# The last down projection as seven products of 2x2 blocks, with its weight sums made in DRAM

## The chip, the cores and the metric

The kernel runs on one core of one Trainium2 chip. A core has a matrix engine (TensorE, PE in the profile; PEld is its loading of the stationary operand), a vector engine (VectorE, DVE), an engine for activations and copies (ScalarE, ACT), a general engine (GpSimd, POOL), an engine that here only issues transfers (SyncE, SP), and 16 DMA engines. The metric is the device time of one execution in microseconds (us), the median of several runs; lower is better.

## What is computed

A two-layer encoder on 272 tokens (16 learned meta tokens and 256 real ones) with 2048 channels, all in float32. Each layer mixes attention with a Fourier branch, then runs a feed-forward block with 5632 inner channels:

```python
for i in range(DEPTH):                                  # DEPTH = 2
    h = _rmsnorm(h_stream, norm_mix[i])
    proj = h @ w_in[i]                                  # q, k, v, f and two gates
    ...                                                 # attention and Fourier branch
    h_stream = h_stream + merged @ w_out[i]

    h2 = _rmsnorm(h_stream, norm_ffn[i])
    up = h2 @ w_up[i]                                   # 2048 -> 2 x 5632
    u_gate = _dwconv3_centred(up[..., :D_FF], w_conv[i], b_conv[i])
    u_val = up[..., D_FF:]
    h_stream = h_stream + (jax.nn.silu(u_gate) * u_val) @ w_down[i]
return h_stream[:, N_META:]                             # the meta tokens are dropped
```

The change concerns `@ w_down[1]`, the very last product. Of its result only the 256 real tokens are wanted.

## The kernel before

Activations are kept channel-major: a tile has 128 channels on the partitions and the tokens along the free dimension. `XT` is the residual stream (16 such tiles). A product is computed as three matmuls in a split format: every float32 operand is cut into a high part in the matrix engine's rounded format (`wh`, `xH`, `gH`) and the rest (`wl`, `xL`, `gL`), and high x high, high x low and low x high are added up in PSUM. Weights are stationary (128 x 128), tokens are moving.

All weights come from DRAM in chunks of 512 KB, 128 partitions x 4 blocks x 256 columns. The list `chunks` holds them in the order of use. For each, SyncE loads a `raw` buffer (four of them), ScalarE casts it to `wh` (`split_w`, L215) and VectorE subtracts to get `wl` (L217); there are three buffers of each, and `advance` keeps two chunks ahead of the one in use (`LOOK`). `group` (L246 to L280) takes the chunks of two output tiles and issues their matmuls: with three matmuls a block (L273 to L275), or, where two copies of the tokens fit into 512 columns, as two (L269: `wh` times high and low tokens side by side, 512 columns; L270: `wl` times high tokens, 256 columns). In layer 1 the value half of the up projection (`ps_uv`) and the down projection (`ps_d`) use the second form.

The small work between (norms, attention, transposes) is written as generators in a list `shadow`. `step()`, called after every second block of a group, lets one of them go on, so that this work is spread among the matmuls; `until` and `drain` force it. A scheduler then places the instructions of each engine: it keeps what the data and the buffers require, and may otherwise move an instruction ahead of others on its engine when it takes it to be ready. Each engine then works through its own list in that order. What must not move is wrapped in `keep_in_program_order`.

```python
def step(force=False):                        # L226
    for s in shadow:
        s[0] -= 1
    for s in list(shadow):
        if force or s[0] <= 0:
            try:
                s[0] = next(s[1])
            except StopIteration:
                shadow.remove(s)
            return
...
def pow_half(out, src):                       # L411
    n = src.shape[1]
    nc.gpsimd.tensor_tensor(out, src, mhalf[:, :n], op=ALU.pow)
```

POOL clears some buffers and takes the inverse square roots of the norms (`pow_half`, L413): `tok` for the norm of all channels, `rk` for the keys, `rq` for the queries, a few values each. VectorE turns `tok` and `rk` into diagonal blocks (`dg` L471, `dk` L829), which TensorE spreads over the partitions, and scales `rq` (L916).

The feed-forward block goes through its inner channels in two parts (`FF_SPLIT`, 24 and 20 tiles). For each pair of tiles: a group `ps_ug`, the convolution and the activation on VectorE and ScalarE, a group `ps_uv`, the product of both, and its split into `gH`, `gL`. After each part come eight groups of the down projection (`ps_d`), whose results VectorE adds to `XT` (L1148, L1154); in the last part of layer 1 the sum goes to a buffer `ot` (L1151) and out to DRAM, channel-major (L1152). While layer 0's feed-forward block runs, another generator (`prefold`) adds and subtracts halves of some weights of layer 1 on VectorE and keeps the results in DRAM (`fw`).

Of the kernel before, what the change touches and what calls it, by code (L numbers as in the profile page):

```python
# [16 lines left out]
P = 128  # L17
# [15 lines left out]
CW = 4  # L33
MG = 2
FF_SPLIT = (24, 20)
F0 = 1536

def _branch(text):
# [87 lines left out]


@with_exitstack
def encoder_kernel(ctx, tc, xT, params, consts, bmat, cfold, csign, w_fl, w_f64c, w_in, w_abr, w_four, w_f64, w_out, w_up, w_down, outT):
# [4 lines left out]

    dram = ctx.enter_context(tc.tile_pool(name="dram", bufs=1, space=bass.MemoryType.DRAM))
    fw = dram.tile([2 * KT, P, CW, MG * P], F32, name="fw")


    IN_F, IN_K, IN_V, IN_Q, IN_GA, IN_GF = 6, 4, 5, 0, 10, 18
    order = []  # L140
    for l in range(DEPTH):
        def g(w, mg, k0, k1):
            return [(w[l, mg, c], CW) for c in range(k0 // CW, k1 // CW)]
        if l == 0:
            f01 = [g(w_in, IN_F + i, 0, KT) for i in range(2)]
            order.append(((l, "f01"), [ch for pr in zip(*f01) for ch in pr]))
            for i in range(2, 4):
                order.append(((l, "f", i), g(w_in, IN_F + i, 0, KT)))
        order.append(((l, "k", 0), g(w_in, IN_K, 0, KT)))
        order.append(((l, "v", 0), g(w_in, IN_V, 0, KT)))  # L150
        for i in range(4):
            order.append(((l, "q", i), g(w_in, IN_Q + i, 0, KT)))
            if l == 1 and i == 1:
                order.append(((l, "f4"), [(fw[kt], CW) for kt in range(KT)]))
        for half in range(2):
            for kind, j in BRANCH_ORDER[half]:
                w, off, n = {"ga": (w_in, IN_GA, KT), "gf": (w_in, IN_GF, KT), "s": (w_four, 0, 8), "a": (w_abr, 0, 8)}[kind]
                chs = [(fw[KT + 2 * j + c], CW) for c in range(2)] if (l, kind) == (1, "s") else g(w, off + j, 0, n)
                order.append(((l, kind, j), chs))
            for mg in range(8):  # L160
                order.append(((l, "o", half, mg), g(w_out, mg, 8 * half, 8 * half + 8)))
        k0 = 0
        for c, n in enumerate(FF_SPLIT):
            for i in range(k0 // MG, (k0 + n) // MG):
                order.append(((l, "ug", i), g(w_up, i, 0, KT)))
                order.append(((l, "uv", i), g(w_up, FT // MG + i, 0, KT)))
            for mg in range(8):
                order.append(((l, "d", c, mg), g(w_down, mg, k0, k0 + n)))
            k0 += n
    chunks = [ch for _, chs in order for ch in chs]  # L170
    folded = {i for i, k in enumerate(k for k, chs in order for _ in chs) if k[:2] == (0, "s")}
    st = {"raw": 0, "fetch": 0, "next": 0, "grp": 0}
    raws, splits = {}, {}
    RAW, LOOK = 4, 2
# [62 lines left out]
    def until(hold, flag):  # L237
        while flag not in hold:
            step(True)

    def drain():
        while shadow:
            step(True)

    def group(key, rhs, width, tag="mm"):
        k, chs = order[st["grp"]]  # L246
        assert k == key, (k, key)
# [2 lines left out]
        ps = [psum.tile([P, 512], F32, tag=tag, name=f"ps_{nm}_{m}") for m in range(MG)]  # L250
        nk = CW * len(chs)
        for j in range(len(chs)):
            i = st["next"]
            advance(i + 1 + LOOK)
            pump(i)
            h, lo = splits.pop(i)
            st["next"] += 1
# [171 lines left out]
    def norm_in(m, goff):  # L429
        norm_split(m, goff)  # L430
        norm_sum(m)

    def prefold(pool):
        src = [w_fl[k] for k in range(KT)] + [w_four[1, j, c] for j in range(NG) for c in range(2)]
        outs = {}
        for j in range(len(src) + 1):
# [13 lines left out]
                outs[j] = o  # L450
            yield 1

    def norm_stats(holder, gap=0):
        am = small.tile([P, P // NM, NM], F32, tag="am", name="am", bufs=1)
        nc.vector.tensor_copy(am, _rep(acc[:, 0:NM], P // NM))
# [22 lines left out]
        holder["tok2"] = tok2  # L478

    xr = lambda lo: (lambda kt: (xH[:, kt, lo:T], xL[:, kt, lo:T]))  # L480

    for l in range(DEPTH):
        last = l == DEPTH - 1
# [615 lines left out]
        with tc.tile_pool(name=f"ffn{l}", bufs=1) as fp:  # L1099
            hold = {}  # L1100
            push(norm_stats(hold), 8)
            if not last:
                push(prefold(fp), 8)
            fused = 2 * W2 <= 512
            k0 = 0
            for c, n in enumerate(FF_SPLIT):
                gHL = fp.tile([P, FF_SPLIT[0], 2, T], F32R, tag="gHL", name="gHL")
                gH, gL = gHL[:, :, 0, :], gHL[:, :, 1, :]
                for i in range(k0 // MG, (k0 + n) // MG):
                    ps = group((l, "ug", i), xr(lo), W)  # L1110
                    until(hold, "tok2")
                    cs = []
                    for m in range(MG):
                        mt = 2 * i + m
                        wc = lambda t: prm[:, P_CW + (l * 3 + t) * FT + mt:P_CW + (l * 3 + t) * FT + mt + 1]
                        bc = prm[:, P_CB + l * FT + mt:P_CB + l * FT + mt + 1]
                        u = fp.tile([P, T], F32, tag="u", name="u", bufs=3)
                        nc.vector.tensor_tensor(u[:, lo:T], ps[m][:, :W], rstdB[:, lo:T], op=ALU.mult)
                        cv = fp.tile([P, T], F32, tag="cv", name="cv", bufs=4)
                        nc.scalar.activation(cv[:, lo2:T], u[:, lo2:T], AF.Identity, bias=bc, scale=wc(1))  # L1120
                        a = max(lo2, 1)
                        nc.vector.scalar_tensor_tensor(cv[:, a:T], u[:, a - 1:T - 1], wc(0), cv[:, a:T], op0=ALU.mult, op1=ALU.add)
                        nc.vector.scalar_tensor_tensor(cv[:, lo2:T - 1], u[:, lo2 + 1:T], wc(2), cv[:, lo2:T - 1], op0=ALU.mult, op1=ALU.add)
                        nc.scalar.activation(cv[:, lo2:T], cv[:, lo2:T], AF.Silu)
                        nc.vector.tensor_tensor(cv[:, lo2:T], cv[:, lo2:T], rstdB[:, lo2:T], op=ALU.mult)
                        cs.append(cv)
                    ps = group((l, "uv", i), (lambda kt: (xHL[:, kt, :, lo2:T],)) if fused else xr(lo2), W2)
                    for m in range(MG):
                        j = 2 * i + m - k0
                        cv = cs[m]  # L1130
                        val = ps[m][:, :W2]
                        if fused:
                            v = fp.tile([P, W2], F32, tag="v", name="v", bufs=2)
                            nc.scalar.copy(v, ps[m][:, W2:2 * W2])
                            nc.vector.tensor_tensor(v, v, val, op=ALU.add)
                            val = v
                        nc.vector.tensor_tensor(cv[:, lo2:T], cv[:, lo2:T], val, op=ALU.mult)
                        nc.scalar.copy(gH[:, j, lo2:T], cv[:, lo2:T])
                        nc.vector.tensor_tensor(gL[:, j, lo2:T], cv[:, lo2:T], gH[:, j, lo2:T].bitcast(F32), op=ALU.subtract)
                lastc = c == len(FF_SPLIT) - 1  # L1140
                for mg in range(8):
                    two = fused and not (lastc and mg == 7)
                    ps = group((l, "d", c, mg), (lambda kt: (gHL[:, kt, :, lo2:T],)) if two
                               else (lambda kt: (gH[:, kt, lo2:T], gL[:, kt, lo2:T])), W2)
                    for m in range(MG):
                        mt = 2 * mg + m
                        if two:
                            nc.vector.tensor_tensor(XT[:, mt, lo2:T], XT[:, mt, lo2:T], ps[m][:, W2:2 * W2], op=ALU.add)  # L1148
                        if last and lastc:
                            ot = fp.tile([P, SEQ], F32, tag="ot", name="ot", bufs=3)  # L1150
                            nc.vector.tensor_tensor(ot, XT[:, mt, NM:T], ps[m][:, :W2], op=ALU.add)  # L1151
                            nc.scalar.dma_start(outT[mt * P:(mt + 1) * P, :], ot)  # L1152
                        else:
                            nc.vector.tensor_tensor(XT[:, mt, lo2:T], XT[:, mt, lo2:T], ps[m][:, :W2], op=ALU.add)  # L1154
                            if lastc:
                                norm_in(mt, P_NM + (l + 1) * KT)
                k0 += n
            drain()


# [62 lines left out]
```

## Time and profile before

| | |
|---|---|
| median of 3 runs | 2576.59 us (2576.39 to 2577.74) |
| profiled execution, its own time | 2576.19 us |
| its span, first to last instruction | 2574.4 us |
| granted TensorE clock, mean | 1.000 |
| TensorE / VectorE / ScalarE / POOL busy | 2564.5 / 1726.7 / 1216.6 / 19.5 us |
| moved by DMA | 499.21 MB, 194 GB/s over the span |
| weight chunks split | 853 from `raw`, and 16 more from folded weights |
| last matmul starts | 2570.60 us |

Durations of matmuls in the profile overlap, since the engine is pipelined; the distance between two starts tells what one costs. A line number is that of the kernel before; in the changed kernel the same statements stand some 30 to 60 lines later. An arrow and a name in square brackets tell what ended an engine's idle time before an instruction.

### The profile page before, as it was taken

To read this page: it belongs to the slowest core of one execution; us is meant where nothing else is said; L and a number is where in the kernel's file an instruction comes from. 1 tells how busy PE (TensorE), PEld (TensorE's weight loads), DVE (VectorE), ACT (ScalarE), POOL (GpSimd) and SP (SyncE) were. 2 spreads that over 40 slices of the span, in tenths; PEclk is the share of its full clock that TensorE was granted. 3 is DMA by queue.
4 is the path that set the end of the run, shared out by engine and by line. 5 is a ranking of instruction groups with operands and counts; after the bars stand their busy time and mean duration, and the time that the engine had idled before them with its cause. 6 is when DMAs were issued, how large, how long until landed. Compare 5 with 4: busy or idle time off the path is not lost. (4 is left out here: it accounts for less than half of the span.)

```text
span 2574.4 us, 47883 instructions
## 1 busy us (share of the span) xinstructions
PE 2564.5 (100%) x19604; PEld 2500.8 (97%) x19604; DVE 1726.7 (67%) x2809; ACT 1216.6 (47%) x1766; POOL 19.5 (1%) x41
## 2 busy tenths in 40 slices
PE   9999999999999999999999999999999999999999
PEld 9999999999999999999999999999999998899988
DVE  7687766776666556666568877667766665566654
ACT  5455534554444334444446555445554443454443
POOL 0000000000000000000000000000000000000000
PEclk9999999999999999999999999999999999999999
DMA  6544555556666666666556445555555555555554
GB/s 235 166 152 160 189 181 186 186 205 223 227 226 225 228 226 227 226 214 218 175 173 221 150 147 197 192 191 196 181 186 184 187 188 188 185 184 188 184 198 158
DMA packets 143100, 499.21 MB, mean 194 GB/s; under 512 B 16400, under 2 KB 23440, under 8 KB 142880
## 3 DMA queue, kind: packets, MB, share of 16 engines
q1 hardware_dynamic: 140432, 494.02, 56.7%
q8 instruction: 153, 2.51, 0.4%
q10 hardware_dynamic: 2448, 2.13, 0.2%
q14 instruction: 67, 0.55, 0.1%
HBM read 474.43 MB, written 18.87 MB: 192 GB/s over the span
## 5 line engine op out<-in xcount | busy, mean ns | idle before, releaser
L217 DVE TENSOR_TENSOR wl<-raw,wh 128x1024 fp32r<-128x1024 f32 (+1 forms) x853 | 1037.7, 1218 | 708.4 <-ACT wh L215 703.0
L215 ACT CAST wh<-raw 128x1024 fp32r<-128x1024 f32 (+1 forms) x853 | 888.8, 1044 | 1052.0 <-issue 164.3
L274 PE MATMUL ps_ug<-xHL,wh 128*128 128x272 f32 (+1 forms) x1408 | 402.4, 286 | 0.0
L273 PE MATMUL ps_ug<-xHL,wh 128*128 128x272 f32 (+1 forms) x1408 | 402.0, 285 | 0.0
L275 PE MATMUL ps_ug<-xHL,wl 128*128 128x272 f32 (+1 forms) x1408 | 401.8, 285 | 0.0
L273 PEld LDWEIGHTS ps_ug<-xHL,wh 128*128 128x128 f32 x1408 | 265.4, 189 | 1.0
L274 PEld LDWEIGHTS ps_ug<-xHL,wh 128*128 128x128 f32 x1408 | 265.5, 189 | 0.1
L275 PEld LDWEIGHTS ps_ug<-xHL,wl 128*128 128x128 f32 x1408 | 265.0, 188 | 0.0
L269 PE MATMUL ps_uv<-xHL,wh 128*128 128x512 f32 x704 | 247.7, 395 | 0.0
L269 PE MATMUL ps_d<-gHL,wh 128*128 128x512 f32 x664 | 233.1, 395 | 0.0
L274 PE MATMUL ps_d<-gHL,wh 128*128 128x272 f32 (+1 forms) x744 | 214.4, 288 | 0.0
L273 PE MATMUL ps_d<-gHL,wh 128*128 128x272 f32 (+1 forms) x744 | 214.1, 288 | 0.0
L275 PE MATMUL ps_d<-gHL,wl 128*128 128x272 f32 (+1 forms) x744 | 214.0, 288 | 0.0
L274 PE MATMUL ps_uv<-xHL,wh 128*128 128x272 f32 x704 | 203.1, 288 | 0.0
L273 PE MATMUL ps_uv<-xHL,wh 128*128 128x272 f32 x704 | 202.9, 288 | 0.0
L275 PE MATMUL ps_uv<-xHL,wl 128*128 128x272 f32 x704 | 202.8, 288 | 0.0
L270 PE MATMUL ps_uv<-xHL,wl 128*128 128x256 f32 x704 | 197.7, 281 | 0.0
L270 PE MATMUL ps_d<-gHL,wl 128*128 128x256 f32 x664 | 186.5, 281 | 0.0
L269 PEld LDWEIGHTS ps_uv<-xHL,wh 128*128 128x128 f32 x704 | 132.4, 188 | 29.9
L269 PEld LDWEIGHTS ps_d<-gHL,wh 128*128 128x128 f32 x664 | 125.0, 188 | 29.2
L273 PE MATMUL ps_ga<-xHL,wh 128*128 128x272 f32 (+1 forms) x512 | 148.2, 289 | 0.0
L273 PE MATMUL ps_gf<-xHL,wh 128*128 128x272 f32 (+1 forms) x512 | 147.3, 288 | 0.0
(323 smaller groups left out, 5850.1 us busy)
## 6 DMA issues: line engine op xcount, KB each, us to landing
raw<-in_w_up SPq DMA_DIRECT2D x352, 512.0 KB, 3.5
raw<-in_w_in SPq DMA_DIRECT2D x191, 512.0 KB, 3.8
raw<-in_w_down SPq DMA_DIRECT2D x176, 512.0 KB, 3.5
raw<-in_w_out SPq DMA_DIRECT2D x64, 512.0 KB, 3.6
raw<-in_w_abr SPq DMA_DIRECT2D x32, 512.0 KB, 3.8
fw<-pfo SPq DMA_DIRECT2D x32, 512.0 KB, 4.3
raw<-fw SPq DMA_DIRECT2D x32, 512.0 KB, 4.3
raw<-in_w_four SPq DMA_DIRECT2D x16, 512.0 KB, 3.9
```

The lines of the kernel that those rows point to most:

```text
L215: nc.scalar.copy(h[:, a:b], r[:, a:b])
L217: nc.vector.tensor_tensor(lo[:, a:b], r[:, a:b], h[:, a:b].bitcast(F32), op=ALU.subtract)
L269: nc.tensor.matmul(o2, h[:, c, sl], ab, start=kt == 0, stop=False)
L270: nc.tensor.matmul(o, lo[:, c, sl], ab[:, 0, :], start=False, stop=kt == nk - 1)
L273: nc.tensor.matmul(o, h[:, c, sl], a, start=kt == 0, stop=False)
L274: nc.tensor.matmul(o, h[:, c, sl], b, start=False, stop=False)
L275: nc.tensor.matmul(o, lo[:, c, sl], a, start=False, stop=kt == nk - 1)
```

## The change

The down projection of layer 1 is no longer computed in two parts by weight-stationary groups.

- **Blocks.** The first 4096 of the 5632 inner channels (`KS` = 32 tiles) are cut in two halves of 16 tiles, the 256 tokens in two halves of 128, and the 2048 output channels in two halves of 1024. Four by four blocks are multiplied by seven products in place of eight, after Strassen and Winograd. Here the tokens are stationary (128 channels x 128 tokens) and the weights are moving, in two matmuls of 512 columns; so the output is token-major.
- **Sums of activations** are made by VectorE in place, and each set of four tiles of an operand is split on both engines when it is wanted (`make`).
- **Sums of weights**, needed in four of the seven products, are made in DRAM (`ft`) by the new generator `weight_sums`: 64 transfers of 1 MB issued by POOL, of which 32 copy and 32 add to what is there. It has a list of its own, `slow`: `step()` counts, starts it after 120 calls, and goes on after 28 more each time. The transfers are not wrapped in `keep_in_program_order`.
- **The rest**, 12 tiles of inner channels, is a plain token-stationary product (`tail`) in four blocks of 512 output columns. The 112 steps of the products (one chunk each) are interleaved: 58 among the chunks of the last six pairs of up tiles, 54 among the 24 chunks of the tail (`mix`).
- The residual is transposed to token-major (`res`) by TensorE during the first up tiles, and the sums are added to it. The output leaves token-major, so that the host no longer transposes it.
- The chunks of layer 1's down projection become 112 + 24 in place of 88. Layer 0 is computed as before.

```diff
+KS = 32
+NQ = KS // 2
+PRODUCTS = (0, 4, 5, 2, 6, 1, 3)
+TAIL_ORDER = (2, 3, 0, 1)
...
+    ft = dram.tile([4, NQ, P, CW, MG * P], F32, name="ft")
...
-        for c, n in enumerate(FF_SPLIT):
+        for c, n in enumerate(FF_SPLIT if l == 0 else (FT,)):
...
+    for b in TAIL_ORDER:
+        order.append(((1, "t", b), [(w_dt[b, j], CW) for j in range((FT - KS) // 2)]))
+    prods = {0: w_dn[0, 0:NQ], 1: w_dn[0, NQ:KS], 2: w_dn[1, NQ:KS], 3: ft[3], 4: ft[0], 5: ft[1], 6: ft[2]}
+    pchunks = [(prods[p][i], CW) for p in PRODUCTS for i in range(NQ)]
+    n_up, n_tail = (FT - KS) // MG * 2 * KT // CW, len(TAIL_ORDER) * (FT - KS) // 2
+    due = lambda t: 58 * t // n_up if t <= n_up else min(58 + (len(pchunks) - 58) * (t - n_up) // (n_tail - 2), len(pchunks))
...
+    slow = [120, None]
+
     def step(force=False):
+        if not force and slow[1]:
+            slow[0] -= 1
+            if slow[0] <= 0:
+                slow[0] = next(slow[1], None)
+                if slow[0] is None:
+                    slow[1] = None
...
+    def weight_sums():
+        rows = lambda ap: ap.rearrange("k p c m -> (k p) (c m)")
+        for j in range(NQ // 2):
+            a, b = 2 * j, 2 * j + 2
+            dst = lambda q: rows(ft[q, a:b])
+            w = lambda h, k: rows(w_dn[h, NQ * k + a:NQ * k + b])
+            for ops in ((((0, w(0, 0)), (2, w(1, 1)), (3, w(0, 1))), None),
+                        (((0, w(1, 0)), (2, w(1, 0))), ALU.add),
+                        (((1, None),), None),
+                        (((1, w(1, 1)),), ALU.add),
+                        (((3, dst(1)),), ALU.add)):
+                for q, src in ops[0]:
+                    if ops[1] is None:
+                        nc.gpsimd.dma_start(dst(q), dst(0) if src is None else src)
+                    else:
+                        nc.gpsimd.dma_start(dst(q), src, accum_op=ops[1], max_dma_last_dim=4096)
+                    yield 28
...
+    slow[1] = weight_sums()
...
+                def products():
...
+                    for n, p in enumerate(PRODUCTS):
+                        ps = [psum.tile([P, 512], F32, tag="aux", name=f"ps_p{p}") for _ in range(2)]
+                        for i in range(NQ):
+                            u = (n * NQ + i) // 4
+                            if i % 4 == 0:
+                                make(u + 2)
+                            wh, wl = (w.rearrange("p c m -> p (c m)") for w in next_split())
+                            a, b = made[u][:, 0, i % 4], made[u][:, 1, i % 4]
+                            for x, w in ((a, wh), (b, wh), (a, wl)):
+                                for h in range(2):
+                                    nc.tensor.matmul(ps[h], x, w[:, 512 * h:512 * h + 512], start=i == 0 and w is wh and x is a,
+                                                     stop=i == NQ - 1 and w is wl)
...
+                for b in TAIL_ORDER:
...
+                            for x, w in ((tH, wh), (tL, wh), (tH, wl)):
+                                nc.tensor.matmul(ps[r][:, :c1 - c0], x[:, kt, tk], w[:, q, c0:c1], start=kt == 0 and x is tH and w is wh,
+                                                 stop=kt == NT - 1 and w is wl)
...
-    args.append(nc.dram_tensor("outT", (D, SEQ), F32, kind="ExternalOutput").ap())
+    args.append(nc.dram_tensor("out", (SEQ, D), F32, kind="ExternalOutput").ap())
```

More of the change, by code (lines that the diff above doesn't have):

```diff
@@ L243, in drain, with next_split @@
             step(True)
+    def next_split():
+        i = st["next"]
+        advance(i + 1 + LOOK)
+        pump(i)
+        st["next"] += 1
+        return splits.pop(i)
     def group(key, rhs, width, tag="mm"):
@@ L252, in group @@
         for j in range(len(chs)):
[L253 to L257, printed above, removed]
+            for _ in range(mix.get((key, j), 0)):
+                next(st["products"])
+            h, lo = next_split()
             cm = [(c, m) for c in range(CW) for m in range(MG)]
@@ L1103, in encoder_kernel, with conv_gate, split_to @@
                 push(prefold(fp), 8)
-            fused = 2 * W2 <= 512
+            def conv_gate(i):
+                ps = group((l, "ug", i), xr(lo), W)
+                until(hold, "tok2")
+                cs = []
+                for m in range(MG):
+                    mt = 2 * i + m
+                    wc = lambda t: prm[:, P_CW + (l * 3 + t) * FT + mt:P_CW + (l * 3 + t) * FT + mt + 1]
+                    bc = prm[:, P_CB + l * FT + mt:P_CB + l * FT + mt + 1]
+                    u = fp.tile([P, T], F32, tag="u", name="u", bufs=3)
+                    nc.vector.tensor_tensor(u[:, lo:T], ps[m][:, :W], rstdB[:, lo:T], op=ALU.mult)
+                    cv = fp.tile([P, T], F32, tag="cv", name="cv", bufs=4)
+                    nc.scalar.activation(cv[:, lo2:T], u[:, lo2:T], AF.Identity, bias=bc, scale=wc(1))
+                    a = max(lo2, 1)
+                    nc.vector.scalar_tensor_tensor(cv[:, a:T], u[:, a - 1:T - 1], wc(0), cv[:, a:T], op0=ALU.mult, op1=ALU.add)
+                    nc.vector.scalar_tensor_tensor(cv[:, lo2:T - 1], u[:, lo2 + 1:T], wc(2), cv[:, lo2:T - 1], op0=ALU.mult, op1=ALU.add)
+                    nc.scalar.activation(cv[:, lo2:T], cv[:, lo2:T], AF.Silu)
+                    nc.vector.tensor_tensor(cv[:, lo2:T], cv[:, lo2:T], rstdB[:, lo2:T], op=ALU.mult)
+                    cs.append(cv)
+                return cs
+            def split_to(h, low, v):
+                nc.scalar.copy(h, v)
+                nc.vector.tensor_tensor(low, v, h.bitcast(F32), op=ALU.subtract)
             k0 = 0
-            for c, n in enumerate(FF_SPLIT):
+            for c, n in enumerate(() if last else FF_SPLIT):
                 gHL = fp.tile([P, FF_SPLIT[0], 2, T], F32R, tag="gHL", name="gHL")
@@ L1109, in encoder_kernel @@
                 for i in range(k0 // MG, (k0 + n) // MG):
[L1110 to L1126, printed above, removed]
@@ L1127, in encoder_kernel @@
-                    ps = group((l, "uv", i), (lambda kt: (xHL[:, kt, :, lo2:T],)) if fused else xr(lo2), W2)
+                    cs = conv_gate(i)
+                    ps = group((l, "uv", i), xr(0), T)
                     for m in range(MG):
                         j = 2 * i + m - k0
[L1130 to L1139, printed above, removed]
@@ L1140, in encoder_kernel @@
-                lastc = c == len(FF_SPLIT) - 1
+                        nc.vector.tensor_tensor(cs[m], cs[m], ps[m][:, :T], op=ALU.mult)
+                        split_to(gH[:, j], gL[:, j], cs[m])
                 for mg in range(8):
-                    two = fused and not (lastc and mg == 7)
-                    ps = group((l, "d", c, mg), (lambda kt: (gHL[:, kt, :, lo2:T],)) if two
-                               else (lambda kt: (gH[:, kt, lo2:T], gL[:, kt, lo2:T])), W2)
+                    ps = group((l, "d", c, mg), lambda kt: (gH[:, kt], gL[:, kt]), T)
```

156 lines of the change are left out of this document (138 added, 18 removed).

## The prediction

> **What bounds the kernel now.** I read the page first (engines, DMA queues, groups), then the busy time by stretches, then the timelines of POOL and VectorE at the start and of TensorE in the last down projection.
>
> ```profile
> PE 2564.5 (100%) x19604; PEld 2500.8 (97%) x19604; DVE 1726.7 (67%) x2809; ACT 1216.6 (47%) x1766; POOL 19.5 (1%) x41
> ...
> q1 hardware_dynamic: 140432, 494.02, 56.7%
> ...
> L217 DVE TENSOR_TENSOR wl<-raw,wh 128x1024 fp32r<-128x1024 f32 (+1 forms) x853 | 1037.7, 1218 | 708.4 <-ACT wh L215 703.0
> L215 ACT CAST wh<-raw 128x1024 fp32r<-128x1024 f32 (+1 forms) x853 | 888.8, 1044 | 1052.0 <-issue 164.3
> ```
>
> TensorE has work throughout; the other engines and the DMA feed it. So the time is TensorE's work plus whatever makes it wait, and today almost nothing does. Two places matter for this change: the last down projection, where its products stand, and the first 125 us, into which the changed program's order puts its weight sums. That start is not idle:
>
> ```profile
> 0.00:3.00 3.00, 0.00 (x0) 0.00 (x0) 0.00 (x0) 1.49 (x2) 2.36 (x15) 1.00 0.39 104
> 3.00:37.00 34.00, 31.81 (x227) 31.49 (x228) 27.30 (x53) 25.11 (x50) 0.51 (x4) 1.00 0.86 298
> 37.00:85.00 48.00, 47.61 (x387) 47.34 (x386) 33.38 (x88) 22.45 (x49) 2.54 (x4) 1.00 0.48 158
> 85.00:123.00 38.00, 38.00 (x303) 37.84 (x303) 27.58 (x48) 17.37 (x26) 0.97 (x1) 1.00 0.55 178
> ```
>
> The last two columns are the busy share of the 16 DMA engines and GB/s. Worked out over the 123 us: 0.39x3 + 0.86x34 + 0.48x48 + 0.55x38 = 74.3 us of all engines busy, 48.7 us free.
>
> POOL does little, but what it does is waited for:
>
> ```profile
> 37.06 1.77 POOL L413 TENSOR_TENSOR tok<-ms,mhalf 128x3 f32<-128x3 f32 x1 [33.42 <-DVE ms L464]
> 84.64 1.33 POOL L413 TENSOR_TENSOR rk<-kss,mhalf 128x6 f32<-128x6 f32 x1 [16.81 <-DVE kss L822]
> 123.43 1.79 POOL L413 TENSOR_TENSOR rq<-qv,mhalf 128x9 f32<-128x9 f32 x1 [37.46 <-DVE qv L897]
> ```
>
> ```profile
> 38.87 0.62 DVE L471 TENSOR_SCALAR dg<-cst,tok 128x16 f32<-128x16 f32 x3 [0.76 <-POOL tok L413]
> 86.01 1.15 DVE L829 TENSOR_SCALAR dk<-cst,rk 128x16 f32<-128x16 f32 x6 [1.44 <-POOL rk L413]
> 125.26 0.17 DVE L916 TENSOR_SCALAR rq<-rq 128x9 f32<-128x9 f32 x1 [1.91 <-POOL rq L413]
> ```
>
> These are the inverse square roots of the norms (`pow_half`). Each time VectorE takes the result within 0.1 us and had nothing else to do before it (idle 0.76, 1.44, 1.91 us): there is no slack. Behind that one waiting instruction on VectorE stand the low-half splits (L217) of all later weights, so TensorE runs dry after the chunks split ahead.
>
> **The change part by part.** *Matmuls.* The old down projection of layer 1:
>
> ```profile
> L269 PE MATMUL ps_d<-gHL,wh 128*128 128x512 f32 x664 | 233.1, 395 | 0.0
> ...
> L270 PE MATMUL ps_d<-gHL,wl 128*128 128x256 f32 x664 | 186.5, 281 | 0.0
> ...
> L273 PE MATMUL ps_d<-gHL,wh 128*128 128x256 f32 x40 | 11.2, 280 | 0.0
> ```
>
> ```profile
> 2479.66 0.40 PE L269 MATMUL ps_d<-gHL,wh 128*128 128x512 f32 x1
> 2479.90 0.28 PE L270 MATMUL ps_d<-gHL,wl 128*128 128x256 f32 x1
> ...
> 2486.68 0.39 PE L269 MATMUL ps_d<-gHL,wh 128*128 128x512 f32 x1
> ...
> 1452.44 0.33 PE ps_pt L962 x3
> ```
>
> Durations overlap, so I take starts: 20 pairs lie between 2479.66 and 2486.68, 0.351 us for 768 columns, so 0.117 for 256 and 0.234 for 512. Removed: 664 x 0.351 = 233.1, and the last group's 40 x 3 x 0.117 = 14.0; together 247.1 us. Added: seven products of 16 chunks of 6 matmuls, 672, and the tail of 12 input tiles by 4 column blocks by 2 token halves by 3, 288: in all 960 x 0.234 = 224.6 us (the last block is cut finer, in equal columns). Eight sets of four transposes bring the residual to token-major: 32 x 0.11 = 3.5. TensorE: 224.6 + 3.5 - 247.1 = **-19.0 us**.
>
> *Feeding the end.* A product needs a 512 KB chunk, split on both engines, for 6 x 0.234 = 1.40 us of TensorE; 136 chunks replace 88.
>
> ```profile
> 2359.04 0.24 PE ps_uv L269
> ...
> 2381.78 0.24 PE ps_uv L269
> ```
>
> ```profile
> L217 DVE TENSOR_TENSOR wl<-raw,wh 128x1024 fp32r<-128x1024 f32 x81 | 99.3, 1226 | 72.9 <-ACT wh L215 72.5
> ```
>
> ```profile
> 2240.00:2470.00 230.00, 230.00 (x1593) 214.53 (x1592) 152.45 (x221) 114.65 (x162) 0.00 (x0) 1.00 0.55 186
> ```
>
> One pair of up tiles takes 22.74 us for 8 chunks. The last six pairs with 58 product steps are 6 x 22.74 + 58 x 1.40 = 217.6 us for 106 chunks. VectorE: 106 x 1.226 = 130, the convolution and gate work of 12 tiles 12 x (152.45 - 99.3)/20 = 32, and some 25 operations of 512 columns on operands and results:
>
> ```profile
> L206 DVE TENSOR_TENSOR wpm<-raw 128x512 f32<-128x512 f32 x32 | 21.1, 688 | 7.8 <-DMA raw<-in_w_four 7.6
> ```
>
> at 0.69, 17: 179 us, 82%. DMA: 106 x 0.524 MB in 217.6 us is 255 GB/s. The tail with 54 steps is 75.6 + 67.4 = 143 us for 78 chunks: VectorE 96 + some 25 = 121 us (85%), DMA 286 GB/s, below the 298 of the stretch from 3 to 37. The averages fit, but three split buffers give two chunks of cover, 2.8 us between two products, for a cast and a subtraction of 1.05 + 1.23 = 2.28. I put 0 to 15 us on it and take 5. The output is still in pieces of at most 128x512 after the last add; no cost. The end gains 19 - 5 = **14 us**.
>
> *Weight sums.* Four of the seven products need sums of weight blocks. `weight_sums` makes them in DRAM by 64 POOL transfers of 1 MB (1.049 MB), 32 copies and 32 accumulations. In the text one is released every 28 steps, but nothing ties a transfer to its step. The changed program's order on POOL has 20 of them ahead of the first root (`tok`), 51 ahead of `rk`, and **all 64 ahead of the first `rq`**. They can't run off freely: an accumulation waits on POOL for the copy into its block, the copy of a sum waits for its accumulation, with mostly three or four transfers from one to the next; the last waits for the one before it. TensorE, VectorE and ACT keep their order there but for a few neighbours. So the root that VectorE took at 125 us comes after 63 transfers have gone through the same 16 DMA engines as the first weights.
>
> The trace of before has no transfer from DRAM to DRAM and none from POOL. Bounds from rows: queue q1 moved 494.02 MB in 56.7% of 2574.4 us, 338 GB/s while busy, so 1.049 MB is 3.10 us of all engines.
>
> ```profile
> raw<-in_w_up SPq DMA_DIRECT2D x352, 512.0 KB, 3.5
> ...
> fw<-pfo SPq DMA_DIRECT2D x32, 512.0 KB, 4.3
> ```
>
> A write to DRAM lands only 0.8 us later than a load of its size, so from below each transfer costs one pass: 63 x 3.10 = 195 us, plus the first weights' 74.3, makes 270; against 123.4 a delay of 146 us. From above every read and write of DRAM is a pass, two for a copy and three for an accumulation: (32x2 + 31x3) x 3.10 = 487, plus 74 is 561, a delay of 438. I take passes by streams read, since a load's write costs no second one: one for a copy, two for an accumulation: (32 + 62) x 3.10 = 291, plus 74.3 is 366, a delay of **242 us**. With two or three transfers queued, 6 to 9 us of work, latency between them is covered.
>
> The Trainium skill ("DMA: Bandwidth & Descriptors", Latency and other measured facts) gives 207 to 214 GB/s for copies between HBM tensors. By an estimate from that page 63 transfers take 63 x 1.049/0.214 = 309 us even if an accumulation costs no more than a copy; the delay is then 260 and the time 2822 us. No run here shows it yet.
>
> Delays at `tok` and `rk` are parts of the same wait, not added to it. Sum against the profiled execution's 2576.19 us (span 2574.4 and 1.8 around it; the median of the runs, 2576.59, is 0.4 higher): 2576.2 - 14 + 242 = **2804 us**.
>
> **Rivals.** *One pass each (0.17).* Accumulations cost no more than copies: 2576.2 - 14 + 146 = 2708. For it: 298 GB/s at 0.86 busy in the start means the engines aren't hurt by load. Against: an accumulation must read its target.
>
> *Every access counts (0.24).* 2576.2 - 14 + 438 = 3000, or between this and the forecast. For it: DRAM both gives and takes these bytes, which no queue here does.
>
> *Late splits (0.07).* Besides the forecast's delay, each product step waits about 0.5 us because a 0.69 us operation on VectorE eats the 2.8 - 2.28 us of cover: 112 x 0.5 = 56 instead of 5, so 2855. Against: up chunks lie between the products.
>
> *Nothing is held up: faster (0.07).* The transfers run beside the weights as the text of the change means them to, or POOL's arithmetic isn't held by the waits of its transfers; then the end's gain alone counts, 2576.2 - 14 = 2562. It decides if `rq` still comes by about 123 + 14 = 137 us: 63 transfers in the 48.7 free us plus 14, 1.0 us each against 3.10 for one pass. So only POOL's arithmetic passing its transfers could do it, and POOL took its instructions of the start in the program's order. The Trainium skill ("DMA: Bandwidth & Descriptors", Issuing engines are not separate DMA queues) says that transfers issued from GpSimd, SP and ACT run on the same 16 engines and interleave. By that rule the transfers can't run beside the weights for nothing; the trace, without POOL transfers, neither shows nor denies it.
>
> **How the numbers follow.** The forecast has 0.45, the rivals 0.17, 0.24, 0.07, 0.07. The range goes from 2690 (the one-pass case with the whole matmul gain and a few us of work done while waiting) to 3000 (every access); outside are the faster rival and some 0.06 of still dearer accumulations or cheaper ones. A measurement of this kernel tells 0.2%, 5 us, from no change: faster 0.06, the rival of that name with little lost at the end; same 0.01; slower 0.93.
>
> **What would show it.** Right: POOL's rows show the first root at about 85 to 110 us instead of 37 and the first `rq` near 366; VectorE idles before L524 and L970 on POOL; TensorE has gaps of tens of us ahead of 370 us and none between there and the last up tiles; the DMA share is near full until then. From the last six up pairs on TensorE takes about 361 us. Wrong in size: a transfer's time from issue to landing, with two or three under way, is far from 6 to 13 us. Wrong altogether: `rq` stays near 125 us, or the transfers stand after the roots. Step by step: starts of 512-column product matmuls 0.234 us apart confirm the matmul term; idle before them on wh or wl, summed, is the 5 us.

## The result, and the profile after

The changed kernel takes **2757.14 us** (median of 4 runs, 2755.35 to 2758.27), the kernel before 2576.49 beside it (4 runs, 2575.43 to 2577.74): a ratio of **1.0701**, 95% interval 1.0688 to 1.0714. The profiled execution took 2756.24 us, with a span of 2754.1. Forecast were 2804 us and a range of 2690 to 3000: the direction and the place were right, and the loss is 181 us where 228 were forecast.

The page of the changed kernel: TensorE and DMA in 40 slices of 69 us, the queues of the weights (q1) and of the weight sums (q0), and the weight sums' copies out of the weights, with their median time from issue to landing (17.4 us).

```profile
PE   4274599999999999999999999999999999999999
...
PEclk7586799999999999999999999999999999999999
DMA  9999845555566666666654554555545555577787
...
q1 hardware_dynamic: 147344, 519.19, 54.7%
q0 software_dynamic: 9728, 67.11, 9.2%
...
ft<-in_w_dn POOLq DMA_DIRECT2D x24, 1024.0 KB, 17.4
```

All the loss stands in the first five slices: the DMA is full and TensorE works about half the time. The three roots on POOL, on the timeline:

```profile
99.50 1.79 POOL L448 TENSOR_TENSOR tok<-ms,mhalf 128x3 f32<-128x3 f32 x1 [5.61 <-DVE ms L517]
...
233.85 1.67 POOL L448 TENSOR_TENSOR rk<-kss,mhalf 128x6 f32<-128x6 f32 x1
...
319.56 2.15 POOL L448 TENSOR_TENSOR rq<-qv,mhalf 128x9 f32<-128x9 f32 x1
```

They stood at 37.06, 84.64 and 123.43. The first and last start of all four `tok` roots, of the kernel before and of the changed one, are in the profile's view of that tile:

```profile
L413 POOL TENSOR_TENSOR tok<-ms,mhalf x4: 848/853/1775, 37.1 to 1830.8; 128x3 f32<-128x3 f32 x4
```

```profile
L448 POOL TENSOR_TENSOR tok<-ms,mhalf x4: 844/852/1792, 99.5 to 2026.4; 128x3 f32<-128x3 f32 x4
```

The last of them is late by 2026.4 - 1830.8 = 195.6 us; the first `rq` already was, by 319.56 - 123.43 = 196.1. So the start costs **196 us** and nothing more is lost until layer 1's feed-forward block. The span grew by 2754.1 - 2574.4 = 179.7, so the end gained **15.9 us**.

The busy time in stretches (PE, PEld, DVE, ACT and POOL busy, then clock, DMA share and GB/s):

```profile
3.00:100.00 97.00, 48.24 (x255) 44.28 (x255) 28.59 (x53) 25.66 (x50) 14.90 (x25) 0.72 1.03 306
100.00:234.00 134.00, 55.20 (x405) 54.16 (x405) 32.90 (x88) 25.54 (x52) 22.62 (x33) 0.69 1.03 289
234.00:320.00 86.00, 47.55 (x309) 45.61 (x309) 27.55 (x49) 15.85 (x25) 11.67 (x18) 0.74 0.97 265
...
350.00:737.00 387.00, 386.40 (x3095) 385.98 (x3094) 287.30 (x506) 189.50 (x301) 0.24 (x1) 1.00 0.53 179
```

Up to 320 us TensorE is busy for 151.0 us with 969 matmuls, 0.156 each; the kernel before needed 117.4 for its 913 up to 123, at a clock of 1.00, 0.129 each. So its work took some 969 x 0.027 = 26 us longer at the clocks of 0.69 to 0.74 in these rows, and for the rest of the 320 us it waited. Whether the 26 us add to the delay, or only fill time in which TensorE would have waited anyway, no run here separates. After 350 us it is busy nearly throughout again.

### The profile page after: what moved, and what is told of

Read it like the earlier page. It is cut to its first block, busy times and chain, and to the rows that moved or that the text cites. A ratio compares the mean times of both kernels' runs of the same rounds, so it can differ in the third digit from the quotient of the medians.

```text
span 2754.1 us, 47402 instructions
## 1 busy us (share of the span) xinstructions
PE 2573.5 (93%) x19184; PEld 2488.8 (90%) x19184; DVE 1789.5 (65%) x2846; ACT 1273.0 (46%) x1820; POOL 64.6 (2%) x105
## 4 chain that ended last, share of the span: by engine, by line
PE 83%; DMA 12%; DVE 2%; issue 1%; POOL 1%; ACT 1%; SPq 0%; ACTq 0%; DVEq 0%; POOLq 0%
DMA ft<-in_w_dn 7%; PE ps_ug L309 6%; PE ps_ug L308 6%; PE ps_ug L310 6%; PE ps_uv L304 6%; PE ps_p L1273 4%; DMA ft<-ft 4%; PE ps_uv L308 3%; PE ps_d L308 3%; PE ps_d L309 3%; PE ps_uv L309 3%; PE ps_uv L310 3%; PE ps_d L310 3%; PE ps_uv L305 3%; PE ps_gf L308 2%; PE ps_gf L309 2%
## 5 line engine op out<-in xcount | busy, mean ns | idle before, releaser
L239 DVE TENSOR_TENSOR wl<-raw,wh 128x1024 fp32r<-128x1024 f32 (+1 forms) x901 | 1093.1, 1218 | 683.6 <-ACT wh L237 678.4
L237 ACT CAST wh<-raw 128x1024 fp32r<-128x1024 f32 (+1 forms) x901 | 938.3, 1044 | 1082.0 <-PE ps_ug L309 194.7
L309 PE MATMUL ps_d<-gHL,wh 128*128 128x272 f32 x704 | 203.1, 289 | 0.0
L308 PE MATMUL ps_d<-gHL,wh 128*128 128x272 f32 x704 | 202.9, 288 | 0.0
L310 PE MATMUL ps_d<-gHL,wl 128*128 128x272 f32 x704 | 202.7, 288 | 0.0
L308 PE MATMUL ps_gf<-xHL,wh 128*128 128x272 f32 (+1 forms) x512 | 147.3, 288 | 0.0
L310 PE MATMUL ps_ga<-xHL,wl 128*128 128x272 f32 (+1 forms) x512 | 146.3, 286 | 0.0
L309 PE MATMUL ps_gf<-xHL,wh 128*128 128x272 f32 (+1 forms) x512 | 146.2, 286 | 0.0
L310 PE MATMUL ps_gf<-xHL,wl 128*128 128x272 f32 (+1 forms) x512 | 146.2, 286 | 0.0
## 6 DMA issues: line engine op xcount, KB each, us to landing
ft<-in_w_dn POOLq DMA_DIRECT2D x24, 1024.0 KB, 17.4
```

The source lines that it names most:

```text
L237: nc.scalar.copy(h[:, a:b], r[:, a:b])
L239: nc.vector.tensor_tensor(lo[:, a:b], r[:, a:b], h[:, a:b].bitcast(F32), op=ALU.subtract)
L308: nc.tensor.matmul(o, h[:, c, sl], a, start=kt == 0, stop=False)
L309: nc.tensor.matmul(o, h[:, c, sl], b, start=False, stop=False)
L310: nc.tensor.matmul(o, lo[:, c, sl], a, start=False, stop=kt == nk - 1)
```

## The experiments

Two theories to begin with. *The queue*: the roots stand behind the transfers on POOL, and whoever frees the roots gets the time back. *Starved weights*: the transfers take the 16 DMA engines from the loads of the weights, whatever stands on POOL. Times are medians beside runs of the kernel before on the same chip (2576.7 to 2578.3 us). Lines left out of a diff are as in the changed kernel.

**The end alone.** No weight sums are made; the four products that need them read other blocks of the same size in their place, so the result isn't the layer's.

```diff
-    prods = {..., 3: ft[3], 4: ft[0], 5: ft[1], 6: ft[2]}
+    prods = {..., 3: w_dn[1, 0:NQ], 4: w_dn[1, 0:NQ], 5: w_dn[0, 0:NQ], 6: w_dn[0, NQ:KS]}
-    slow[1] = weight_sums()
```

> The changed kernel without the weight sums: the four products that need them read other blocks of the same weights, so that the traffic and the matmuls of the end are the same and the result of these four is not. Every theory: the start is as before the change, first rq of layer 0 near 125 us, and the whole gain of the end is left, 2576.5 - 16 = 2560, 2555 to 2564. The distance from e1_in_order is what 64 transfers cost when they are spread. Theory of the end: above 2575.

Measured: **2561.34 us**, ratio 0.9943 (0.9927 to 0.9960), span 2559.1. The products and their feeding gain 15 us, and all of the loss is the sums': 2757.1 - 2561.3 = 196 us. This kernel is the yardstick for the rest.

**The transfers in their written order.**

```diff
-                        nc.gpsimd.dma_start(dst(q), ...)
+                        tc.keep_in_program_order(nc.gpsimd.dma_start(dst(q), ...))
```

(and so for the accumulating line)

> The changed kernel with its 64 weight-sum transfers kept in program order on POOL, so that each stands where its step releases it, one about every 18 us, and only a few ahead of any root. Theory of the queue (the roots stood behind the transfers on POOL, and the delay is the DMA work ahead of the last of them): the 196 us of the start vanish, and the time is 2557 to 2575, most likely 2563. Theory of the starved weights (the transfers take the DMA engines from the first weights; where the roots stand doesn't matter): spread over layer 0 they take 253 us of DMA time out of a stretch that is half free, so here too the delay vanishes, to about 2565. Theory of the end (the seven products are fed too slowly, and the start is only part of it): above 2590. This run doesn't tell the first two apart; it tells whether the arrangement of the transfers is the whole loss.

Measured: **2660.43 us**, ratio 1.0319 (1.0303 to 1.0334): 99 us above the kernel without sums, where 2563 was expected. The first roots are on time now, `tok` at 40.3 and `rq` at 126.7. The stretches show where the time goes:

```profile
150.00:265.00 115.00, 107.48 (x840) 105.88 (x838) 78.81 (x181) 53.74 (x104) 15.46 (x20) 0.99 0.96 282
265.00:568.00 303.00, 294.19 (x2329) 293.82 (x2330) 214.63 (x343) 139.78 (x206) 0.70 (x1) 0.98 0.60 192
568.00:805.00 237.00, 197.04 (x1374) 189.16 (x1373) 112.97 (x178) 78.09 (x101) 25.72 (x38) 0.91 1.01 312
```

An order fixes what a transfer stands behind, not when it starts. Nothing on POOL takes time between two roots, so the transfers between them run off at once: until 265 us, and, after POOL has waited 307.8 us for the next `tok`, from 568 to 805, with the DMA full and TensorE idle for 40 us. The release every 28 steps is a place in the text, no pace.

**Copies in place of accumulations**, to price an accumulation; the sums are not formed, 64 blocks are only copied.

```diff
-                        nc.gpsimd.dma_start(dst(q), src, accum_op=ops[1], max_dma_last_dim=4096)
+                        nc.gpsimd.dma_start(dst(q), src)
```

> The changed kernel with each of the 32 accumulating transfers replaced by a copy of the same size into the same place (the sums are then not sums). Theory of the queue with the price by streams read, as the packets of the changed kernel give it (2.56 us of all engines for a copy, 5.35 for an accumulation): 63 x 2.56 + 74 = 235 us until the first rq, a delay of 112 in place of 196, so 2757 - 84 = 2673, 2655 to 2690. Rival, a price of latency (each transfer in the chain of waits costs its 15 to 17 us from issue to landing whatever its kind): the delay stays near 196, 2740 to 2760.

Measured: **2725.13 us**, ratio 1.0574 (1.0553 to 1.0595), between the two. The delay is 164 us where 112 were expected from a copy's 2.56 us. A part of the difference is the price: here the 64 copies alone took 6.9% of all engines over 2723.3 us, by the packet records 2.95 us each, so 63 x 2.95 + 74 - 123 = 137. The rest is no root behind a transfer: POOL issues the last one at 265.67 and then waits 20.57 us for the root's input, which VectorE makes from products of the weights:

```profile
286.73 1.82 POOL L448 TENSOR_TENSOR rq<-qv,mhalf 128x9 f32<-128x9 f32 x1 [20.57 <-DVE qv L951]
```

So the queue on POOL, even at its measured price, isn't the whole of it.

**Roots off POOL.** The inverse roots are taken by ScalarE and VectorE, so that nothing of the layer's own work stands behind the transfers, save the clearing of a few buffers.

```diff
-        nc.gpsimd.tensor_tensor(out, src, mhalf[:, :n], op=ALU.pow)
+        nc.scalar.activation(out, src, AF.Sqrt)
+        nc.vector.reciprocal(out, out)
```

> The changed kernel with its transfers where they are, but the roots taken by ScalarE (square root) and VectorE (reciprocal) in place of POOL, so that no root stands behind a transfer. Theory of the queue: VectorE and TensorE no longer wait for POOL; what is left is that transfers and first weights share the engines, which costs the start that needs 0.86 of them alone some 20 to 50 us, and a few us for the tables of ScalarE: 2575 to 2620, most likely 2600. Theory of the starved weights: the delay is that of the changed kernel, 2730 to 2760.

Measured: **2738.63 us**, ratio 1.0627 (1.0605 to 1.0648). The queue theory, which the prediction rests on, falls as the sole cause: with no root behind a transfer, and no wait of VectorE, ScalarE or TensorE for POOL in the first 350 us, 177 of the 196 us stay.

Back in the trace of the changed kernel, VectorE and ScalarE around the first root show the other cause at work:

```profile
98.08 1.04 ACT L237 CAST wh<-raw 128x1024 fp32r<-128x1024 f32 x1
108.53 0.85 ACT L676 CAST br<-cst 32x276 fp32r<-32x276 f32 x2 [9.41 <-DMA cst<-in_consts]
122.75 0.42 ACT L672 CAST BH<-bt 128x276 fp32r<-128x276 f32 x1 [13.37 <-DMA bt<-in_bmat]
123.08 1.04 ACT L237 CAST wh<-raw 128x1024 fp32r<-128x1024 f32 x1
134.22 0.40 ACT L320 CAST w<-r 64x256 fp32r<-64x256 f32 x1 [10.10 <-DMA r<-in_w_f]
```

```profile
134.65 0.42 DVE L321 TENSOR_TENSOR w<-r,w 32x256 fp32r<-32x256 f32 x1 [34.11 <-ACT w L320]
135.10 0.62 DVE L524 TENSOR_SCALAR dg<-cst,tok 128x16 f32<-128x16 f32 x3
```

`tok` was ready at 101.3, but `dg` came at 135.1: what held it was not POOL but a small piece of weights ahead of it on VectorE, which ScalarE had to convert first; and ScalarE waited 9 to 13 us three times over for constants and weights from the DMA. For the two later roots the waits list (us in all, times, longest) does name POOL:

```profile
PE ps_nb L527 <- DVE dg L524: 44.5, 1, 44.5
...
DVE dk L883 <- POOL rk L448: 47.2, 2, 46.0
...
DVE rq L970 <- POOL rq L448: 23.4, 3, 20.0
```

**Smaller packets.** The copies move rows of 64 KB as single packets, the accumulations are cut to 4 KB, and a packet of the weights' queue q1 lasts 0.16 us on average against a copy's 2.56. If the engines take turns between queues by the packet, the copies win by size. So the same limit is set for the copies, first alone, then with the roots off POOL.

```diff
-                        nc.gpsimd.dma_start(dst(q), dst(0) if src is None else src)
+                        nc.gpsimd.dma_start(dst(q), dst(0) if src is None else src, max_dma_last_dim=4096)
```

> The changed kernel with its 32 copies cut into rows of 4 KB, as the accumulations are, in place of 64 KB (the bytes, the order on POOL and the waits stay). Three theories now. Queue: the roots behind the transfers set the time, first rq when weights and sums are through, 74 + 250 us: unchanged, 2745 to 2765. Shares: the engines take packets of the queues in turn, so that a weight packet of 4 KB (0.16 us) stands behind a 64 KB packet of a copy (2.56 us) and gets 6% of the engines during copies, and a third during accumulations; that alone would give back some 55 us here (half of the engines during copies), 2690 to 2715, unless the queue holds it up. Volume: any 253 us of transfers in a full DMA delay the weights alike, whatever the packets: unchanged, 2745 to 2765.

> e5_roots_on_ACT with the copies cut into rows of 4 KB as well: neither roots behind transfers nor large packets. Shares: the transfers last until about 420 us in place of 330, the weights get 166 us of the engines by then in place of 77, and the delay shrinks from 177 to about 120 us: 2665 to 2705. Volume: unchanged, 2730 to 2750. Queue alone (which e5_roots_on_ACT spoke against): unchanged.

Measured: the cut alone **2760.42 us**, ratio 1.0712 (1.0692 to 1.0731), nothing gained; with the roots off POOL as well **2657.97**, ratio 1.0314 (1.0295 to 1.0333), 81 us less than with the roots off POOL alone and 7 below the range expected of the shares. So there are two locks, and either alone holds the time: POOL's roots behind the transfers, and the loads of weights behind large packets. Undo both and half the delay goes.

The waits show which lock holds each kernel. These are from the list of the cut copies alone:

```profile
ACT wh L237 <- DMA raw<-in_w_in: 18.5, 12, 4.0
...
DVE dk L883 <- POOL rk L448: 92.0, 2, 90.8
...
DVE rq L970 <- POOL rq L448: 35.7, 3, 32.2
```

And for all five, summed up to 325 us, with VectorE's waits for `dg`, `dk` and `rq`:

| kernel | VectorE waits for POOL's roots | ScalarE waits for loads of `in_w_in` |
|---|---|---|
| changed | 66.0 us | 89.2 us |
| copies only | 5.0 | 130.1 |
| roots off POOL | none | 90.5 |
| cut copies | 135.7 | 18.0 |
| both | none | 25.0 |

With the roots off POOL in both, smaller packets take the waits for these weights from 90.5 to 25.0 us. With the roots on it they fall too, but VectorE then waits twice as long for POOL. Freeing the roots alone takes those waits away and leaves the waits for weights as they were.

One account fits all five kernels whose transfers run from the start. The rows below are the stretch from 0 to the end of the last transfer's packets, of the changed kernel, then of copies only, roots off POOL, cut copies, and both:

```profile
0.00:326.40 326.40, 154.25 (x983) 147.32 (x984) 93.67 (x196) 69.79 (x133) 53.24 (x86) 0.71 1.01 284
```

```profile
0.00:273.40 273.40, 135.21 (x825) 129.58 (x826) 79.42 (x173) 61.62 (x121) 37.69 (x85) 0.74 0.94 326
```

```profile
0.00:340.70 340.70, 196.76 (x1261) 188.19 (x1262) 127.93 (x284) 96.31 (x184) 47.77 (x83) 0.78 1.01 289
```

```profile
0.00:327.10 327.10, 144.24 (x984) 140.66 (x985) 93.95 (x196) 70.10 (x133) 54.24 (x86) 0.72 1.01 284
```

```profile
0.00:378.40 378.40, 310.29 (x2241) 305.20 (x2242) 223.66 (x477) 160.65 (x297) 49.68 (x83) 0.90 1.03 312
```

and the kernel without sums, at four times:

```profile
0.00:108.00 108.00, 103.19 (x805) 102.63 (x806) 78.09 (x172) 60.97 (x120) 6.37 (x21) 1.00 0.60 205
0.00:127.00 127.00, 122.19 (x957) 121.63 (x958) 91.63 (x194) 68.53 (x129) 8.17 (x22) 1.00 0.61 202
0.00:164.00 164.00, 159.19 (x1254) 158.52 (x1255) 124.71 (x274) 89.05 (x174) 9.96 (x23) 1.00 0.58 191
0.00:286.00 286.00, 280.78 (x2231) 279.90 (x2232) 220.77 (x471) 153.32 (x289) 9.96 (x23) 1.00 0.55 179
```

Take the last column times the stretch, less the 67.1 MB of the sums: that is what else was moved, nearly all weights. The kernel without sums has moved as much at the time in the third column; the difference of the times is the delay that should result. The last column is the measured difference of the spans.

| kernel | weights moved by then | without sums at | difference | span less 2559.1 |
|---|---|---|---|---|
| changed | 284 x 0.3264 - 67.1 = 25.6 MB | 127 us | 199 us | 195 us |
| copies only | 326 x 0.2734 - 67.1 = 22.0 | 108 | 165 | 164 |
| roots off POOL | 289 x 0.3407 - 67.1 = 31.4 | 164 | 177 | 181 |
| cut copies | 284 x 0.3271 - 67.1 = 25.8 | 127 | 200 | 198 |
| both | 312 x 0.3784 - 67.1 = 51.0 | 286 | 92 | 97 |

So in all five the delay is what the weights still lacked when the sums were through. The account holds whichever lock kept them back; it says what the delay is made of, and the waits above tell the locks apart. The sums get 67 of 93 MB in the changed kernel; with both locks undone the weights get twice as much in a stretch 52 us longer.

The Trainium skill ("DMA: Bandwidth & Descriptors", Queues, rings and completion order) says that each DMA engine goes round its queues and drains a whole packet of one before it takes the next. The step from 31.4 to 51.0 MB, by smaller packets alone once no root waits on POOL, agrees with it. The turns themselves, and whether what the Trainium skill calls a packet is one of this profile's, no run here shows.

**A pace.** What the text of the change lacks is something that makes a transfer wait. Here VectorE copies one column of the newest `wl`, POOL copies that, and the transfer follows in POOL's order; so it can't start before its step. First with the copies whole, then cut to 4 KB rows.

```diff
+            last_low[0] = lo
...
+    def pace():
+        a = small.tile([P, 1], F32, tag="pace", name="pace", bufs=4)
+        nc.vector.tensor_copy(a, last_low[0][:, 0, 0:1].bitcast(F32))
+        b = small.tile([P, 1], F32, tag="paced", name="paced", bufs=4)
+        tc.keep_in_program_order(nc.gpsimd.tensor_copy(b, a))
...
+                    pace()
-                        nc.gpsimd.dma_start(dst(q), ...)
+                        tc.keep_in_program_order(nc.gpsimd.dma_start(dst(q), ...))
```

> The changed kernel with each transfer tied to its step: VectorE copies one column of the newest low half, POOL copies that and only then issues the transfer, all kept in order; so a transfer goes out about every 18 us through layer 0, one or two under way, and none can run ahead. All three theories: no root stands behind more than one transfer, DMA is about 0.77 busy, the raw buffers cover a hold-up of some 10 us. 2558 to 2572, most likely 2564: faster than the kernel before by about 0.5%. If 64 KB packets stall weights even one at a time: above 2580. If the loss were anything but the bunching of transfers: above 2620.

> e8_paced with the copies cut into rows of 4 KB. Shares: a copy no longer holds up the weights, so equal to e8_paced or a few us below, 2558 to 2568. Volume and queue: equal to e8_paced.

Measured: **2574.78 us**, ratio 0.9992 (0.9983 to 1.0001), and **2573.77**, ratio 0.9987 (0.9978 to 0.9996). The 196 us are gone but for 13 and 12, and both kernels lie above what was expected (2572 and 2568 at most). Of the 12 some 9 stand as gaps on TensorE: 4 between 100 and 300 us, 5.2 in one gap at 1387. The timelines of POOL and of VectorE in the second kernel around it:

```profile
1371.60 0.95 POOL L512 DMA_DIRECT2D ft<-in_w_dn  x1
```

```profile
1387.24 0.72 DVE L858 TENSOR_TENSOR qs<-qs,cst 128x544 f32<-128x544 f32 x1 [5.07 <-DMA qs<-qp]
```

VectorE waits 5.07 us, with the splits of the weights behind it, for `qs<-qp`, four small transfers that SyncE issued from 1378.4 on (they exchange halves of the queries for the rotation). An accumulation of 1 MB is issued at 1371.6; by the packet records its packets run from 1374.1 to 1383.0, and those of `qs<-qp` only from 1382.1 to 1386.2. So here it is no root that waits; it is a small transfer that shares the DMA with a large one.

**The pace away from attention.** The first transfer only after about 340 us, and a pause after the fortieth that takes in the attention of layer 1.

```diff
-    slow = [120, None]
+    slow = [400, None]
...
-                    yield 28
+                    count[0] += 1
+                    yield 28 * 18 if count[0] == 40 else 28
```

> The paced transfers with 4 KB rows, but none of them near an attention: the first only after about 340 us, and a pause of some 380 us after the fortieth, so that both layers' roots for the queries stand outside the transfers. Without any sums the time was 2561.3; the paced kernel with 4 KB rows stood 12.4 above that, 2.1 + 1.8 us of it as gaps of TensorE between 100 and 300 us and 5.2 as one gap at 1387. If the rest of the loss comes from where the transfers stand, these gaps go and 2559 to 2565 us come out, 0.5% faster than before. If 67 MB of transfers cost some 12 us wherever they stand, 2570 to 2576, as before.

> The same places and pauses with the copies left in packets of 64 KB. If the packet size only matters where the queue of transfers is full, with one transfer every 21 us it does nothing: within 2 us of the same kernel with 4 KB rows, 2559 to 2567. If each 64 KB packet still delays a weight load by itself, 2567 to 2576.

Measured: **2564.06 us**, ratio **0.9952** (0.9938 to 0.9965), with 4 KB rows, and **2566.00**, ratio 0.9957 (0.9945 to 0.9970), with whole ones: both faster than the kernel before, by 0.5%, and 3 to 5 us above the kernel without sums. Where transfers come one by one, these runs show no effect of the packet size: the intervals overlap. The issues of the first, its copies from the weights:

```profile
L511 POOL DMA_DIRECT2D ft<-in_w_dn x24: 552/567/763, 336.6 to 1950.2; - x24
...
DMA to landing us min/median/max: 5.5/8.3/10.3
```

With no transfer near, VectorE's wait for `qs<-qp` is 0.25 us at the same place:

```profile
1382.90 0.73 DVE L860 TENSOR_TENSOR qs<-qs,cst 128x544 f32<-128x544 f32 x1 [0.25 <-DMA qs<-qp]
```

The gap at 1387 has shrunk to 0.4 us. One of 3.5 is left, at 470 us; VectorE waits 7.4 us there for a load of `in_w_four`. That a weight sum delays this load too is likely, but was not tried.

## Why the prediction was right, and what in it was wrong

*TensorE's work and the feeding of the end* held: +14 forecast, 15.9 in the changed kernel, 15 by the kernel without sums. The starts of 512-column matmuls are closer than forecast. On the timeline of the tail:

```profile
2604.30 0.40 PE L1334 MATMUL ps_t<-wh,tH 128*128 128x512 f32 x1
...
2606.82 0.39 PE L1334 MATMUL ps_t<-wl,tH 128*128 128x512 f32 x1
```

Eleven steps in 2.52 us are 0.229 against 0.234, which makes 960 of them 5 us cheaper. From 2389 us on TensorE's waits for `wh` and `wl` sum to 2.8 us against 5. The last six pairs and the tail took 364 us (2386.1 to 2750.4), where 361 and the 5 of waits were forecast; so most of the 7 us that these two terms saved went elsewhere in this stretch, and where was not traced. The rival *late splits* is out: 56 us of such waits aren't there.

*The order on POOL* held: 20 transfers ahead of `tok`, 51 ahead of `rk`, all 64 ahead of `rq`; `tok` at 99.5 (85 to 110 forecast), the first `rq` after the last transfer but at 319.6 in place of 366. *The DMA as the pace of the start* held as well: full until the last transfer, 74 us of first weights and the passes of the sums one after the other.

*The term that was mis-sized is the price of a pass.* I took 3.10 us, from queue q1's bytes over its busy time, 338 GB/s. In the packet records of q0 the 32 copies are 512 packets of 64 KB with 2.555 us each, over 16 engines 2.56 us a copy; the 32 accumulations are 8192 packets of 4 KB with 0.334, so 5.35 us. The rule, one pass for a copy and two for an accumulation, fits (2.09 times); the pass is 2.6 to 2.7 us in this kernel. With these prices the prediction's own sum is 32 x 2.56 + 31 x 5.35 + 74.3 = 322 us, and `rq` is taken at 321.7. That is 44 of the 46 us by which the delay was too large. The rivals *one pass each* and *every access counts* fall with the ratio.

The Trainium skill ("DMA: Bandwidth & Descriptors", Latency and other measured facts) has 207 to 214 GB/s for copies between HBM tensors, measured on 128 rows of 16 KiB that lie 512 KiB or more apart. Here, in packets of 64 KB, 1.049 MB in 2.56 us of all engines is 410 GB/s, and the measurement decides.

*The reason for the delay was only half of it.* The prediction saw the roots held on POOL and took the weights for served once they had their 74 us. With the measured prices the sum comes out right, and this is partly luck: in the changed kernel both locks open at nearly the same time. The root's input was there at about 301.6, POOL took it at 319.6, and at 326 us the DMA has given the weights 25.6 MB, which is what the kernel without sums has moved at 127, when `rq` is due. The prediction expected VectorE to idle on POOL ahead of L524; it idled on a starved load. Freeing the roots, at which the queue theory puts the whole delay, gave back 19 us. The step that failed is the one from the order on POOL to the wait: ahead of `dg` VectorE waited for a load held up in the DMA, and over the start ScalarE waited 89 us for loads of `in_w_in`, where VectorE waited 66 for POOL.

*Nothing is held up* (2562, with 0.07) didn't come true, but its number is what the change is worth when the sums don't collide: 2561.3 without them, 2564.1 with them spread.

*Time from issue to landing* was forecast at 6 to 13 us with two or three under way, and was 17.4 and 15.4. Spread, in packets of 4 KB, a copy takes 8.3; whole, 7.4. I had this as a mark of a wrong size alone. How much of the 17.4 is the weights in between, and how much the transfers' own neighbours in the queue, no run separates.

## What to carry to other kernels

A transfer that nothing waits for still needs a reason to start late: a place in the text, even an order kept by force, is no pace. Tie it to a piece of data that exists only at that step. When such traffic delays the start, ask for both locks, what stands behind it on the issuing engine and what it takes from the loads, since removing one alone can show nothing. And price the delay in bytes: what the loads got until the bulk was through, against when they would have had it without.

## What the runs showed of the hardware that was not expected

An accumulating transfer of 1.049 MB from DRAM to DRAM took 5.35 us of all engines, 2.09 times the 2.56 of a copy beside it; where there were only copies, each took 2.95. Cutting copies into 4 KB packets left the transfers' own total nearly as it was (9.5% of 2656.2 us against 9.3% of 2740.3) and gave the weights 51.0 in place of 31.4 MB. And in the stretches in which TensorE waited for weights and roots its mean granted clock was 0.69 to 0.74, and a matmul took 0.156 us on average where 0.129 did before; what that cost in time is not shown.
